# Where the last blocks of a Mamba layer hand over to its scans: order of work, an immediate finish, row-shaped decays, and square sums in a shared bank

## The chip, the cores and the metric

The kernel runs on one core of a Trainium2 chip. The metric is the device time of one execution in microseconds (us). Five engines work side by side and each takes its own instructions in order: TensorE (PE in the profile, PEld for its weight loads), VectorE (DVE), ScalarE (ACT), GpSimd (POOL) and SyncE (SP). SP, ACT and POOL also issue DMA transfers; in the profile these stand as SPq, ACTq and POOLq.

## The reference

Two layers over 1024 tokens of width 1024, each with a norm ahead of it and a residual, and a last norm. Layer A is a chunked causal spatial gating MLP, layer B a Mamba-2 mixer. The change lies in layer B:

```python
proj = h @ w_in
z, xbc, dt_raw = split(proj)
xbc = silu(causal_depthwise_conv(xbc, conv_w, conv_b))     # 4 taps
x, Bm, Cm = split(xbc)
dt = softplus(dt_raw + dt_bias);  dA_cs = cumsum(dt * A, axis=chunk)
decay = exp(where(causal, dA_cs[l] - dA_cs[s], -inf))
w_ls = (Cm @ Bm.T) * decay * dt
y_diag = w_ls @ x
states = Bm.T @ (exp(dA_cs[-1] - dA_cs) * dt * x)
state  = state * exp(dA_cs[-1]) + states                   # from chunk to chunk
y = y_diag + (Cm @ state_before) * exp(dA_cs) + x * d_skip
gated = rmsnorm_per_group(y * silu(z))                     # 8 groups of 256 channels
out = gated @ w_out
```

There are 8 groups of 4 heads of 64 channels, 128 states, and 8 chunks of 128 tokens. All is float32.

## The kernel before, in words

Every product in float32 is made of three passes (`mm3`, L134 to L136): an operand is split into a rounded part (`wh`, `hh`, a cast on ScalarE, L111) and a rest (`wl`, `hl`, a subtraction, mostly on VectorE, L112).

Most of layer B's input projection is done in blocks (`Block`), each a two by two product by Strassen-Winograd's scheme: seven smaller products in the order 1, 2, 6, 7, 5, 4, 3 instead of eight. A product needs one operand prepared (`prep`, which casts and subtracts), then TensorE fills a PSUM bank (tile `acc`), and `post` passes it on. Products 1, 6 and 7 are copied to `u` by ScalarE (L292), and the next product that goes on in the same bank waits for that copy. Products 2, 5, 4 and 3 complete the quarters C11, C22, C21 and C12, which go to the block's `done`.

The blocks of layer B are run by `blocks()`: a list `bs` of seven, of which the last is `zb[3]`, half as wide as the others (one unit for each product). For a z block, `done` adds on VectorE (L960), and a function `rest` applies SiLU on ScalarE (L965) and stores to `z_d` from ScalarE's queue (L966). C21 has no addition: its SiLU reads PSUM. For an xbc block, `done` puts a convolution into the list `todo`. A convolution is one activation on ScalarE (L1275), three taps on VectorE (L1269, with small extra taps at L1272 for the columns before), and as its `rest` a SiLU (L1300) and a store (L1301) on ScalarE.

`unit(b, n, i)` is one unit of a product. It takes what is in `late`, may pop one convolution from `todo` (whose `rest` goes into `late`), issues the matmuls and their `post`, and then runs what it took from `late`. So a SiLU normally comes one unit after the work that it needs. `finish()` runs all of `late` at once; before the change only block 0 calls it.

Four groups are not in blocks (`plain`: 2, 4, 6, 7). Their projections come from the generator `projections()`: straight products of four by two by two matmul triples into a double PSUM bank (`ab`). Its first `next` issues the first weight loads, then `prep(0, 0)` and `prep(0, 1)` split that weight, and the matmuls follow, two triples for each `next`. `prep` also issues the loads of the next weight, and from the second weight on subtracts on GpSimd.

`scans()` follows, with a new set of PSUM banks (`new_psum`): chunk by chunk and group by group, with pieces of the plain projections (`project`) between. In chunk n it issues `pe_b` of n (tiles `yy`, `sp`), `pe_a` of n + 2 (tile `tp`), then the updates, the weights of n + 1, the decay of n + 2, and the load of n + 3 (`wl<-cs_d`, one row of 4 heads by 128 to all partitions). `prefetch` loads half a group's x, B, C, its z, and in four DMAs the exponentials of the decays (`ze<-ecs_d`). For the group norm, `squares`, `sum_a`, `sum_b` and `sum_c` stand in the four chunks after a half is done: squares on ScalarE, a sum on GpSimd, sums over partitions on TensorE by a column of ones (tile `pr`, L1624) with a copy by ScalarE (tile `srow`, L1628), and a store by SP (L1631). The small PSUM tiles `yy`, `sp`, `tp` and `pr` share four banks.

The instructions inside `into_b()`, `blocks()` and `scans()` keep, on each engine, the order in which they are written (`tc.manual_schedule()`). What stands outside, such as the `next(pj)` between `blocks()` and `new_psum`, is placed by the scheduler at a time that it works out, and the lists of `blocks()` and `scans()` may also interleave where they meet.

Of the kernel before, what the change touches and what calls it, by code (L numbers as in the profile page):

```python
# [8 lines left out]
F32 = mybir.dt.float32  # L9
# [6 lines left out]
P = 128  # L16
T = 1024
# [6 lines left out]
NH = 32  # L24
# [5 lines left out]
def kernel(  # L30
# [921 lines left out]
    def z_block(b):  # L952

        wide = 256 if b < 3 else 128

        def done(name, i, a, u):
            th, j = 2 - int(name[1]), int(name[2]) - 1
            zt = k2([P, 512], "zt")
            if u is not None:
                nc.vector.tensor_tensor(out=zt, in0=a, in1=u, op=ALU.add)  # L960
                a = zt
            g, m = (2 * b + j, i) if b < 3 else (6, j)

            def rest():
                nc.scalar.activation(zt, a, AF.Silu)  # L965
                nc.scalar.dma_start(out=z_d[g][:, m, th * 512:(th + 1) * 512], in_=zt)  # L966

            late.append(rest)
            if not b:
                finish()  # L970

        def W(kh, j):
            c = 512 * b + j * wide
            return [b_w_in[kh * 512:(kh + 1) * 512, c:c + wide]]

        return Block(H2, W, False, done, None, wide)
# [31 lines left out]

    SPILT, AHEAD, LEFT = (0, 1, 3, 5), 16, 3
    zb = [z_block(b) for b in range(4)]  # L1010
# [181 lines left out]
    cs_d = dr.tile([8, NH, P], F32, name="cs_d")  # L1192
    ecs_d = dr.tile([8, NH, P], F32, name="ecs_d")

    def decays():
# [35 lines left out]
        for q in range(4):  # L1231
            rs_ = slice(q * 32, (q + 1) * 32)
            for sc, src in ((cs_d, cs), (ecs_d, ecs)):
                nc.sync.dma_start(out=sc[2 * q:2 * q + 2].rearrange("c h l -> h c l"),
                                  in_=src[rs_, :].rearrange("h (c l) -> h c l", c=2))
            yield
# [104 lines left out]
    def projections():  # L1341
# [37 lines left out]
        for kh in range(2):  # L1379
            prep(0, kh)  # L1380
        yield
        last = 0
        for i, (g, kind) in enumerate(seq):
            for m in range(2):
                drain(len(queue) - last)
                ab = acc2("ab")
                for kh in range(2):
                    for th in range(2):
                        for k in range(4):
                            mm3(ab[:, th, :], [w[:, k, m * P:(m + 1) * P] for w in W[i, kh]],  # L1390
                                [h_[:, k, :] for h_ in H2[f"A{2 - th}{kh + 1}"]], kh == 0 and k == 0,
                                kh == 1 and k == 3)
                            if (kh, th, k) == (1, 1, 3):
                                last = push(g, kind, m, ab)
                            if k % 2:
                                yield
                    if (m, kh) == (0, 1):
                        prep(i + 1, 0)
                    elif (m, kh) == (1, 0):
                        prep(i + 1, 1)  # L1400
# [3 lines left out]
    def blocks():  # L1404
# [11 lines left out]
        def unit(b, n, i):  # L1416

            turn[0] += 1
            off = late[:]
            late.clear()  # L1420
            if next(small, 0) == 0 and todo and (turn[0] % 2 or len(todo) > 3):
                late.append(todo.pop(0)())
            b.mm(n, i)
            for f in off:
                f()

        for at, (k, n) in enumerate(seq[1:], 1):
# [19 lines left out]
            elif n == 6:  # L1447
                next(pj)
            elif n == 7:
                next(a21)  # L1450
            elif n == 4:
                next(a21, None)
            for i in range(b.units):
                unit(b, n, i)
        while len(todo) > LEFT:
            convolve()

# [30 lines left out]
    def prefetch(g, th):  # L1488
# [8 lines left out]
        for f in range(2):  # L1497
            for pt in range(2):
                nc.sync.dma_start(
                    out=ze[f * 64:(f + 1) * 64, 2 + pt].rearrange("p (c l) -> p c l", c=4),  # L1500
                    in_=ecs_d[4 * th:4 * th + 4, 4 * g + 2 * pt + f, :].partition_broadcast(64))

    class Scan:
# [54 lines left out]

        def pe_b(self, c):
            w, wl = self.cw[c], self.wl.pop(c)  # L1560
# [5 lines left out]
            if c > 0:  # L1566
                for pt in range(2):
                    nc.tensor.matmul(out=yy[:, 256 + pt * P:384 + pt * P],  # L1568
                                     lhsT=self.state[c - 1][:, pt * P:(pt + 1) * P], rhs=self.x(3, c),
                                     start=True, stop=True)  # L1570
            sp = None
            if c < 7:
                sp = sm("sp")
                nc.tensor.matmul(out=sp[:, 0:256], lhsT=w[:, 512:640], rhs=w[:, 256:512], start=True, stop=True)
            self.ps[c] = yy, sp

# [41 lines left out]

        def sum_b(self):
            pr = sm("pr")  # L1620
            n = 1 if self.g < G - 1 else 2
# [62 lines left out]
    def scans():  # L1684
# [33 lines left out]
        for n, (g, c) in enumerate(chunks):  # L1718
            want = lambda f: AHEAD + (total - AHEAD) * (n + f) // N
            at("pe_b", n)  # L1720
            project(want(.5))
# [10 lines left out]
            at("load", n + 3)  # L1732
            p = g if c >= 4 else g - 1
            th = 0 if c >= 4 else 1
            if p >= 0:
# [3 lines left out]
                elif c % 4 == 1:  # L1739
                    sc.sum_a()  # L1740
                elif c % 4 == 2:
                    sc.sum_b()
                else:
                    sc.sum_c(th)
# [186 lines left out]
```

## Time and profile before

| | |
|---|---|
| median of 3 runs | 1622.55 us (1622.11 to 1625.1) |
| profiled execution | 1620.58 us, span 1618.9 us |
| TensorE busy | 1507.8 us (93%) |
| VectorE, ScalarE, GpSimd busy | 1056.2, 775.8, 458.4 us |
| DMA | 187256 packets, 259.17 MB |
| blocks of layer B | up to about 1050 us |
| scans with plain projections | about 1058 to 1400 us |

In a row of a timeline the columns are: start in us, duration in us, engine, line, operation, output tile <- input tiles, shapes, count. In brackets stands how long the engine was idle before the row and what, by the profile, ended that. A row with x2 or more merges several instructions, and its duration is theirs together. In a row of waits: who waited for whom, the total in us, how often, and the longest. A row of the table of windows gives the stretch, its length, the busy us (and instructions) of PE, PEld, DVE, ACT and POOL, then the granted TensorE clock as a share of full speed, the DMA share and GB/s.

### The profile page before, as it was taken

Reading aid. Unit: us, or ns where it says so; the run is one execution under the profiler, and the core shown is the slowest. Engines: PE = TensorE matmul, PEld = TensorE weight load, DVE = VectorE, ACT = ScalarE, POOL = GpSimd, SP = SyncE. Lnnn points to the kernel's source line nnn. Section 1 sums busy time; section 2 is a strip of 40 time slices with the busy share of each in tenths; the row PEclk is TensorE's granted clock in tenths of the full one; section 3 lists DMA queues with packets and bytes.
Section 4 is the critical chain, followed back from the end, with each engine's and each line's share of the span. In section 5 each row is a group of like instructions: output and inputs, shape, how many; then the busy total and the mean of one; then the engine's idle time right before and its main releaser. Section 6 shows DMA issues by size and latency. Waiting matters only on the chain.

```text
span 1618.9 us, 21275 instructions
## 1 busy us (share of the span) xinstructions
PE 1507.8 (93%) x7834; PEld 1241.1 (77%) x7834; DVE 1056.2 (65%) x1684; ACT 775.8 (48%) x1248; POOL 458.4 (28%) x466
## 2 busy tenths in 40 slices
PE   5799999999999999997999999889999999969987
PEld 5799988888888878775788787667767777747776
DVE  7966566666666545577737377747767667658656
ACT  4522233232323345554655555536666676444444
POOL 3601110000000131235311312026766666221231
PEclk8999999999999999998999999999999999979989
DMA  5153323323334999932377878766666765795992
GB/s 171 42 193 134 106 92 110 108 99 107 109 109 164 303 263 237 195 101 64 102 163 173 169 162 153 200 175 191 159 159 165 185 179 141 244 235 168 228 238 107
DMA packets 187256, 259.17 MB, mean 160 GB/s; under 512 B 16288, under 2 KB 117392, under 8 KB 183952
## 3 DMA queue, kind: packets, MB, share of 16 engines
q1 hardware_dynamic: 134144, 166.30, 34.0%
q0 software_dynamic: 39808, 70.53, 22.3%
q10 hardware_dynamic: 13200, 20.98, 3.6%
q8 instruction: 62, 1.02, 0.2%
q14 instruction: 42, 0.34, 0.1%
HBM read 183.52 MB, written 51.18 MB: 145 GB/s over the span
## 4 chain that ended last, share of the span: by engine, by line
PE 57%; issue 15%; DMA 10%; DVE 8%; ACT 7%; POOL 1%; SPq 1%; ACTq 0%; POOLq 0%; DVEq 0%
PE acc L136 10%; PE acc L134 9%; PE acc L135 9%; DMA wl<-cs_d 4%; PE ab L134 3%; PE ab L136 3%; PE ab L135 3%; PE ao L135 3%; PE ao L134 3%; PE ao L136 3%; PE yy L1564 2%; PE yy L1568 2%; DVE wl L112 2%; DVE xc L1269 2%; DMA wb<-in_b_w_out_dram 1%
## 5 line engine op out<-in xcount | busy, mean ns | idle before, releaser
L134 PE MATMUL acc<-hh,wh 128*128 128x512 f32 x868 | 343.4, 396 | 9.4 <-ACT wh L111 7.5
L136 PE MATMUL acc<-hh,wl 128*128 128x512 f32 x868 | 341.2, 393 | 4.9 <-DVE wl L112 4.8
L135 PE MATMUL acc<-hl,wh 128*128 128x512 f32 x868 | 340.1, 392 | 0.0
L112 DVE TENSOR_TENSOR wl<-wr,wh 128x1024 fp32r<-128x1024 f32 (+1 forms) x99 | 120.9, 1223 | 128.2 <-ACT wh L111 128.1
L134 PEld LDWEIGHTS acc<-hh,wh 128*128 128x128 f32 x868 | 164.5, 189 | 46.4 <-ACT wh L111 9.6
L136 PEld LDWEIGHTS acc<-hh,wl 128*128 128x128 f32 x868 | 164.4, 189 | 43.3 <-DVE wl L112 8.7
L135 PEld LDWEIGHTS acc<-hl,wh 128*128 128x128 f32 x868 | 164.5, 189 | 33.3
L111 ACT CAST wh<-wr 128x1024 fp32r<-128x1024 f32 (+1 forms) x113 | 116.4, 1030 | 98.0 <-PE acc L135 56.5
L292 ACT COPY u<-acc 128x512 f32<-128x512 f32 x117 | 67.7, 584 | 194.9 <-PE acc L136 193.7
L136 PE MATMUL acc<-wh,hl 128*128 128x256 f32 x448 | 130.2, 291 | 12.4 <-DVE hl L395 12.4
L134 PE MATMUL acc<-wh,hh 128*128 128x256 f32 x448 | 131.0, 292 | 3.8 <-DVE vt L331 2.5
L135 PE MATMUL acc<-wl,hh 128*128 128x256 f32 x448 | 129.6, 289 | 1.3 <-DVE wl L405 1.3
L134 PE MATMUL ab<-hh,wh 128*128 128x512 f32 x256 | 116.5, 455 | 8.7 <-ACT xc L1300 8.7
L1538 ACT ACTIVATE wl<-wl,tk 128x128 f32<-128x128 f32 x256 | 82.1, 391 | 84.9 <-DMA wl<-cs_d 84.5
L136 PE MATMUL ab<-hh,wl 128*128 128x512 f32 x256 | 101.6, 397 | 0.0
L135 PE MATMUL ab<-hl,wh 128*128 128x512 f32 x256 | 101.0, 395 | 0.0
L136 PEld LDWEIGHTS acc<-wh,hl 128*128 128x128 f32 x448 | 88.9, 198 | 13.5 <-DVE hl L395 13.5
L134 PE MATMUL bo<-wh,xh 128*128 128x512 f32 x192 | 80.5, 419 | 16.1 <-ACT xh L111 11.9
L134 PEld LDWEIGHTS acc<-wh,hh 128*128 128x128 f32 x448 | 88.8, 198 | 4.8 <-issue 2.9
L112 DVE TENSOR_TENSOR xl<-ya,xh 128x1024 fp32r<-128x1024 f32 x40 | 48.9, 1224 | 65.7 <-ACT xh L111 65.7
L135 PEld LDWEIGHTS acc<-wl,hh 128*128 128x128 f32 x448 | 88.8, 198 | 1.7 <-DVE wl L405 1.5
L111 ACT CAST xh<-ya 128x1024 fp32r<-128x1024 f32 x40 | 42.1, 1051 | 94.4 <-PE ao L135 43.0
(323 smaller groups left out, 3328.9 us busy)
## 6 DMA issues: line engine op xcount, KB each, us to landing
wr<-in_a_w_in_dram SPq DMA_DIRECT2D x48, 512.0 KB, 3.8
wl<-cs_d SPq DMA_DIRECT2D x64, 256.0 KB, 7.1
wr<-in_b_w_in_dram SPq DMA_DIRECT2D x30, 512.0 KB, 4.0
ya<-ya POOLq DMA_DIRECT2D x28, 512.0 KB, 15.0
wb<-in_a_w_out_dram SPq DMA_DIRECT2D x10, 1024.0 KB
wb<-in_b_w_out_dram SPq DMA_DIRECT2D x10, 1024.0 KB, 13.0
wr<-in_b_w_in_dram SPq DMA_DIRECT2D x36, 256.0 KB, 8.8
v<-v_d SPq DMA_DIRECT2D x8, 1024.0 KB, 4.8
```

What stands on the lines that cost most here:

```text
L111: nc.scalar.copy(out=hi, in_=src)
L112: return (eng or nc.vector).tensor_tensor(out=lo, in0=src, in1=hi.bitcast(F32), op=ALU.subtract)
L134: nc.tensor.matmul(out=o, lhsT=l[0], rhs=r[0], start=start, stop=False, **kw)
L135: nc.tensor.matmul(out=o, lhsT=l[0], rhs=r[1], start=False, stop=False, **kw)
L136: nc.tensor.matmul(out=o, lhsT=l[1], rhs=r[0], start=False, stop=stop, **kw)
L292: nc.scalar.copy(out=self.u[n][:, i], in_=a)
L1269: nc.vector.scalar_tensor_tensor(dst[:, s:], src[:, :n - s], convw(3 - s, ch), dst[:, s:], ALU.mult, ALU.add)
L1538: nc.scalar.activation(wl[:, j, :], wl[:, j, :], AF.Relu, scale=-1.0, bias=tokc(2, c, self.g)[:, j:j + 1])
L1564: nc.tensor.matmul(out=yy[f * 64:(f + 1) * 64, pt * P:(pt + 1) * P], lhsT=w[:, j * 64:(j + 1) * 64], rhs=wl[:, j, :], start=True, stop=True)
L1568: nc.tensor.matmul(out=yy[:, 256 + pt * P:384 + pt * P], lhsT=self.state[c - 1][:, pt * P:(pt + 1) * P], rhs=self.x(3, c), start=True, sto ...
```

## The change

There are five edits.

- `finish()` is now also called for z block 3, so that each of its four `rest` functions, and whatever else is in `late`, is issued at once.
- In the last block's products 4 and 3 no convolution is popped, and the loop that emptied `todo` down to three at the end of `blocks()` is gone. What is left is issued by the loop in `scans()`.
- `projections()` yields after each of the first two splits, and `blocks()` calls it once more at the last block's product 3, so the first split of the first plain weight is now issued there, in the written order. The second split stays at the `next(pj)` after the blocks. The two halves of the tokens are multiplied in the order 1, 0 instead of 0, 1.
- `ecs_d` is laid out as one row of 1024 for each head. Each load of `prefetch` now takes one run of 512 values instead of four runs of 128.
- `sum_b` is called from `pe_b` of the next chunk and puts its sums into the upper half of the state's bank (`sp`) instead of a bank of its own. In chunk 7, which has no state, `sp` is taken for it.

```diff
@@ z_block
             late.append(rest)
-            if not b:
+            if b in (0, 3):
                 finish()
@@ layer B
-    SPILT, AHEAD, LEFT = (0, 1, 3, 5), 16, 3
+    SPILT, AHEAD = (0, 1, 3, 5), 16
...
-    ecs_d = dr.tile([8, NH, P], F32, name="ecs_d")
+    ecs_d = dr.tile([NH, T], F32, name="ecs_d")
@@ decays
-            for sc, src in ((cs_d, cs), (ecs_d, ecs)):
-                nc.sync.dma_start(out=sc[2 * q:2 * q + 2].rearrange("c h l -> h c l"),
-                                  in_=src[rs_, :].rearrange("h (c l) -> h c l", c=2))
+            nc.sync.dma_start(out=cs_d[2 * q:2 * q + 2].rearrange("c h l -> h c l"),
+                              in_=cs[rs_, :].rearrange("h (c l) -> h c l", c=2))
+            nc.sync.dma_start(out=ecs_d[:, q * 256:(q + 1) * 256], in_=ecs[rs_, :])
@@ projections
         for kh in range(2):
             prep(0, kh)
-        yield
+            yield
...
-                    for th in range(2):
+                    for th in (1, 0):
...
-                            if (kh, th, k) == (1, 1, 3):
+                            if (kh, th, k) == (1, 0, 3):
                                 last = push(g, kind, m, ab)
@@ blocks
-            if next(small, 0) == 0 and todo and (turn[0] % 2 or len(todo) > 3):
+            if b is bs[-1] and n in (4, 3):
+                pass
+            elif next(small, 0) == 0 and todo and (turn[0] % 2 or len(todo) > 3):
                 late.append(todo.pop(0)())
...
             elif n == 4:
                 next(a21, None)
+            elif n == 3:
+                next(pj)
             for i in range(b.units):
                 unit(b, n, i)
-        while len(todo) > LEFT:
-            convolve()
@@ prefetch
-                nc.sync.dma_start(
-                    out=ze[f * 64:(f + 1) * 64, 2 + pt].rearrange("p (c l) -> p c l", c=4),
-                    in_=ecs_d[4 * th:4 * th + 4, 4 * g + 2 * pt + f, :].partition_broadcast(64))
+                h = 4 * g + 2 * pt + f
+                nc.sync.dma_start(out=ze[f * 64:(f + 1) * 64, 2 + pt],
+                                  in_=ecs_d[h, th * 512:(th + 1) * 512].partition_broadcast(64))
@@ Scan.pe_b
-        def pe_b(self, c):
+        def pe_b(self, c, ends=None):
...
+            if c < 7 or ends is not None:
+                sp = sm("sp")
             if c < 7:
-                sp = sm("sp")
                 nc.tensor.matmul(out=sp[:, 0:256], lhsT=w[:, 512:640], rhs=w[:, 256:512], start=True, stop=True)
+            if ends is not None:
+                ends.sum_b(sp[:, 256:512])
@@ Scan.sum_b
-        def sum_b(self):
-            pr = sm("pr")
+        def sum_b(self, pr=None):
+            pr = sm("pr") if pr is None else pr
@@ scans
-            at("pe_b", n)
+            p = g if c >= 4 else g - 1
+            at("pe_b", n, scan[p] if c % 4 == 3 and p >= 0 else None)
...
-                elif c % 4 == 2:
-                    sc.sum_b()
-                else:
+                elif c % 4 == 3:
                     sc.sum_c(th)
```

More of the change, by code (lines that the diff above doesn't have):

```diff
@@ L1732, in scans @@
             at("load", n + 3)
-            p = g if c >= 4 else g - 1
             th = 0 if c >= 4 else 1
```

## The prediction

> **What bounds the kernel now.** I read the page's span and busy times first, then TensorE's own waits, then the timeline around the two places that the change touches.
>
> ```profile
> span 1618.9 us, 21275 instructions
> PE 1507.8 (93%) x7834; PEld 1241.1 (77%) x7834; DVE 1056.2 (65%) x1684; ACT 775.8 (48%) x1248; POOL 458.4 (28%) x466
> ...
> 1040.00:1058.00 18.00, 9.38 (x39) 6.71 (x37) 14.58 (x22) 10.22 (x14) 2.83 (x1) 0.90 1.07 325
> ...
> PE ab L134 <- ACT xc L1300: 8.7, 1, 8.7
> ```
>
> TensorE is busy for 93% of the span, so time is only to be had where it stands still. The table of windows has one such stretch: in 1040 to 1058, TensorE works 9.38 of 18 us (first pair of numbers) while VectorE works 14.58 (third). The waits of TensorE there name one stop of 8.7 us, ahead of the first plain projection (tile `ab`). The releaser named, a SiLU of ScalarE, writes no PSUM; VectorE's rows show the real one:
>
> ```profile
> 1046.78 1.91 ACT L111 CAST hh<-f 128x2048 fp32r<-128x2048 f32 x1 [2.77 <-DMA f<-f_d]
> ...
> 1048.72 2.29 DVE L112 TENSOR_TENSOR hl<-f,hh 128x2048 fp32r<-128x2048 f32 x1 [1.52 <-ACT hh L111]
> 1050.93 2.35 DVE L112 TENSOR_TENSOR wl<-wr,wh 128x1024 fp32r<-128x1024 f32 x2
> 1053.32 2.72 DVE L1269 SCALAR_TENSOR_TENSOR xc<-u,par,xc 128x511 f32<-128x511 f32 x1
> ...
> 1057.66 0.68 DVE L960 TENSOR_TENSOR zt<-acc,u 128x512 f32<-128x512 f32 x1
> ...
> 1058.49 0.77 PE L134 MATMUL ab<-hh,wh 128*128 128x512 f32 x1 [8.68 <-ACT xc L1300]
> 1059.06 0.63 PE L135 MATMUL ab<-hl,wh 128*128 128x512 f32 x1
> ...
> 1061.19 0.45 PE L134 MATMUL ab<-hh,wh 128*128 128x512 f32 x1
> 1061.47 0.40 PE L135 MATMUL ab<-hl,wh 128*128 128x512 f32 x1
> 1061.71 0.40 PE L136 MATMUL ab<-hh,wl 128*128 128x512 f32 x1
> ```
>
> The last product of the blocks ended at 1049.8. Its reader L960 ends at 1058.34 and `ab` starts 0.15 later, in the PSUM that L960 frees. L960 stands on VectorE behind the split of A21, two weight splits and one convolution. The first six matmuls of `ab` take 2.70 us (1058.49 to 1061.19) where six at the later step of about 0.23 take 1.4: a slow clock adds 1.3.
>
> **The change at the seam, step by step.** With no convolution in products 4 and 3, the last convolution (from 1053.32 to L960, 4.3 us of VectorE) goes behind the first `ab` products. Its cost there is nothing, and what hides it is VectorE's idle time:
>
> ```profile
> 1072.24 3.92 DVE L1269 SCALAR_TENSOR_TENSOR x<-ab,par,x 128x1023 f32<-128x1023 f32 x3 [13.89 <-ACT x L1275]
> ```
>
> 13.9 us stand empty there; without them it would cost its 4.3 us. Its SiLU and store go the same way on ScalarE; group 5 reads it much later. The moved split `prep(0, 0)` issues one cast, one VectorE subtract and two SyncE loads, now ahead of product 3's reader, as they already stood; `prep(0, 1)` is free to fall behind L960, and is needed only 24 matmuls (5.4 us) into `ab`. The order (1, 0) of the halves saves nothing: A21 is split by 1051.0, before `ab` could start. By these steps alone L960 would follow the first split: 1048.72 + 2.29, half of 2.35, 0.68, so 1052.9, and `ab` would start at 1053.0, 5.5 us sooner.
>
> Against this stands the `finish()` for block 3. It runs everything in `late` at once, and that includes the SiLU of the convolution just issued in the same unit. ScalarE is in order, so it now stands still until VectorE has made the three taps. What is queued behind it there:
>
> ```profile
> 1034.35 0.62 ACT L1300 ACTIVATE xc<-xc 128x512 f32<-128x512 f32 x1
> ...
> 1035.37 0.62 ACT L111 CAST wh<-wr 128x512 fp32r<-128x512 f32 x1 [0.40 <-ACT xc L1300]
> 1035.90 0.81 ACT L1275 ACTIVATE xc<-u,par 128x512 f32<-128x512 f32 x1
> 1036.61 0.59 ACT L292 COPY u<-acc 128x512 f32<-128x512 f32 x1
> 1037.10 0.64 ACT L1300 ACTIVATE xc<-xc 128x512 f32<-128x512 f32 x1
> ...
> 1038.19 0.63 ACT L965 ACTIVATE zt<-zt 128x512 f32<-128x512 f32 x1 [0.46 <-DVE wl L112]
> ...
> 1039.22 0.62 ACT L111 CAST wh<-t 128x512 fp32r<-128x512 f32 x1 [0.40 <-ACT zt L965]
> ...
> 1034.48 2.31 DVE L1269 SCALAR_TENSOR_TENSOR xc<-acc,par,xc 128x511 f32<-128x511 f32 x3 [0.51 <-ACT xc L1275]
> 1036.72 0.68 DVE L960 TENSOR_TENSOR zt<-acc,u 128x512 f32<-128x512 f32 x1
> ...
> 1037.25 0.50 PE L134 MATMUL acc<-hh,wh 128*128 128x512 f32 x1 [0.68 <-ACT u L292]
> ```
>
> These are units 2 and 6 of the last z block. Today's order is: SiLU of an older convolution, cast for product 7, convolution, copy `u` (L292, which releases product 7 at 1037.25), and only then the SiLU of unit 2's convolution and of z. After the change it is: SiLU of unit 2's convolution (taps end 1036.79, so 1036.89), z's SiLU one step of 1.09 later (1037.98), the older SiLU (+1.03, 1039.01), the cast (+1.02, 1040.03), convolution (+0.53), copy (+0.71, 1041.27, done 1041.86). Product 7 starts at 1041.9 instead of 1037.25: **4.65 us late**, and after 5 us of standing still its first seven matmuls are slow (as after the stop at 1058).
>
> From there the chain is ScalarE and VectorE alone. Product 7 is done at 1046.2 (seven steps of 0.43, four of 0.23, 0.39); copy 0.5, SiLU 1.0, cast 0.5, convolution 0.8 bring the taps of unit 5 to 1049.15. Those taps last
>
> ```profile
> 1043.54 0.75 DVE L1269 SCALAR_TENSOR_TENSOR xc<-u,par,xc 128x511 f32<-128x511 f32 x1
> ...
> 1045.79 0.22 DVE L1272 SCALAR_TENSOR_TENSOR xc<-halo,par,xc 128x3 f32<-128x3 f32 x1
> ```
>
> 2.47, so to 1051.6. Then the second wait in line: SiLU 1051.7, z's SiLU 1052.8, cast for product 3 1053.85, cast of A21 1054.35 to 1056.25, its subtract 2.29 to 1058.6, the first split 1.18 to 1059.75, L960 0.68, `ab` at **1060.5**. That is 2.0 later than 1058.49, although the convolution is gone; 0.7 later if `ab` then starts at full clock. TensorE's stop there would be 2.7 us, behind another of 2.8 ahead of product 3. Rows for whether shorter stops slow the clock:
>
> ```profile
> 1014.77 0.50 PE L134 MATMUL acc<-hh,wh 128*128 128x512 f32 x1 [1.48 <-ACT wh L111]
> ...
> 1016.03 0.50 PE L136 MATMUL acc<-hh,wl 128*128 128x512 f32 x1 [0.53 <-DVE wl L112]
> ...
> 1017.18 0.63 PE L134 MATMUL acc<-hh,wh 128*128 128x512 f32 x1
> ```
>
> Stops of 1.48 and 0.53 were followed by slow matmuls too, so I give the slow clock 6 in 10 and take +1.5 for the seam. The ends are -5.5 (the waits in line cost nothing) and +3.7 (below).
> The Trainium skill (TensorE: Matmul & The Clock Gate, Part 1: The HAM clock gate) has TensorE fall to half clock after an idle window of about 3.4 us. By that rule a stop of 2.7 us leaves it warm and the seam is +0.7; the row at 1017.18 does not agree with it, and I keep +1.5.
>
> **The change in the scans.** Here TensorE has two stops of about 3 us. One of them, with SyncE's queue ahead of it:
>
> ```profile
> 1063.85 0.94 SPq L1527 DMA_DIRECT2D wl<-cs_d  x2
> ...
> 1194.36 2.60 SPq L1499 DMA_DIRECT2D ze<-ecs_d  x4
> 1197.06 0.55 SPq L1527 DMA_DIRECT2D wl<-cs_d  x1
> ...
> 1197.20 0.60 PE L1624 MATMUL pr<-gsq,ones 128*1 128x256 f32 x4
> ...
> 1204.83 1.28 ACT L1538 ACTIVATE wl<-wl,tk 128x128 f32<-128x128 f32 x4 [8.32 <-DMA wl<-cs_d]
> ...
> 1206.80 0.69 DVE L1556 TENSOR_TENSOR wl<-wl,cw 128x512 f32<-128x512 f32 x1 [4.57 <-ACT wl L1540]
> 1206.82 0.73 ACT L1628 COPY srow<-pr 1x256 f32<-1x256 f32 x2
> ...
> 1207.59 0.72 PE L1564 MATMUL yy<-wl,cw 128*64 128x128 f32 x8 [3.41 <-ACT srow L1628]
> ...
> 1294.86 0.66 PE L1564 MATMUL yy<-wl,cw 128*64 128x128 f32 x8 [2.94 <-ACT srow L1628]
> ...
> DMA to landing us min/median/max: 6.7/7.1/23.5
> ```
>
> The profile names the copy of the square sums, ended at 1207.55. But the weights of the same products ended at 1207.49, behind a decay that waited 8.32 us for its load. So moving the sums into the state's bank is worth 0.06 us at each of the stops it is named for: 0.2 in all, taken as nothing. It adds no wait here: the new place is behind the products that end near 1201.5, five before the copy. Elsewhere the copy may make ScalarE wait some tenths, covered by a decay that runs a chunk ahead; unhidden over 14 sums that would be up to 3.
>
> What counts is the load: it left SyncE at 1197.06, behind four `ecs_d` loads of 0.65 us each. One row of 2 KB per partition is the form of the `cs_d` loads, 0.47 each (0.94 for two). Four save 0.7. The load landed after 7.8; the last row, of the `cs_d` loads, has 6.7 at best and 7.1 in the middle; I take 7.1, so another 0.7. Ends: 0 (nothing lands sooner) and 0.7 + 1.1 = 1.8. Two stops times 1.4 are **-2.8**; next late is still the same load, since 3.41 - 1.4 leaves 2.0. The smaller copies into `ecs_d` lie among the blocks and change nothing.
>
> **Sum.** +1.5 - 2.8 - 0.2 = -1.5. Against the profiled execution (1620.58, of which 1618.9 is span) that is 1619.1; the median of the runs shown stands 1.97 above it, so **1621.0**.
>
> **Rivals.** (a) The waits in line are hidden and the seam closes as its first steps say: -5.5 - 3.0, 1614.0, and 1.3 less with a warm clock. For it: removing the 4.3 us is certain. Against it: L292 stands behind the SiLUs on an in-order engine. (b) The merged rows do not land or issue sooner: the seam alone, 1622.55 + 1.5 = 1624.0. For it: the cs_d loads, already in this form, still need 6.7 at best. The Trainium skill (DMA: Bandwidth & Descriptors, Specifications) calls 512 B enough for line rate, which speaks for this. (c) Slower: `prep(0, 1)`, which is outside the hand-written order, is placed ahead of A21's cast or of L960. Two casts and splits already stand before L960 today (2.35 for two), so it costs a cast of 1.0 and a split of 1.2 on the chain: seam +3.7 to +4.2. It decides once the loads give less than 0.5; with none, 1626.5.
>
> **Chances.** My forecast 0.60 (own range 1618 to 1624), (a) 0.17, (b) 0.13, (c) 0.10. No change is what lies within 0.2% (3.2 us), about what a measurement can tell. A fifth of the first case, where both loads land 1.8 sooner, lies below 1619.3 and counts with (a): faster 0.29, slower 0.10, same 0.61. The range goes to (a) with a slow or half warm clock, 1613.5, and nearly to (c), 1626.0.
>
> **What would show it.** Right: in the last z block a stop of about 5 us ahead of product 7, released by L292, with ScalarE waiting on a tap; `ab` near 1060; `ecs_d` issues near 0.47; the two stops in the scans at 1.5 to 2.0; the copy no longer named. Wrong: product 7 still near 1037 and `ab` near 1053, or the stops in the scans unchanged.

## The result and the profile after

| | before | after |
|---|---|---|
| median of 5 runs | 1622.55 us (1622.0 to 1626.07) | 1616.14 us (1611.99 to 1624.39) |
| ratio of the runs, 95% interval | | 0.9948 [0.9932, 0.9964] |
| profiled execution, span | 1620.58, 1618.9 us | 1619.06, 1617.4 us |

The changed kernel is faster by 0.5%. The forecast was 1621.0 us, with a chance of 0.61 for no change beyond 0.2% and of 0.29 for faster. The time lies inside the range as a whole (1613.5 to 1626.0) but below the 1618 to 1624 of the forecast's own case, and by the forecast's own 0.2% it is faster. The profiled execution of after is one of the longer of its five: it is 1.5 us shorter than that of before, where the medians are 6.4 us apart. The page of after:

```profile
span 1617.4 us, 21264 instructions
PE 1510.1 (93%) x7834; PEld 1243.0 (77%) x7834; DVE 1059.3 (65%) x1684; ACT 775.4 (48%) x1248; POOL 460.4 (28%) x466
...
DMA packets 174840, 259.17 MB, mean 160 GB/s; under 512 B 16288, under 2 KB 100880, under 8 KB 171536
```

Work and bytes are the same as before; only packets fell, from 187256, by the merged rows of `ecs_d`.

The seam, from TensorE's timeline of after (the bracket is the stop ahead of the row):

```profile
1015.81 0.50 PE L134 MATMUL acc<-hh,wh 128*128 128x512 f32 x1 [1.17 <-ACT wh L111]
...
1041.32 0.80 PE L134 MATMUL acc<-hh,wh 128*128 128x512 f32 x1 [4.84 <-ACT u L292]
...
1055.07 0.50 PE L134 MATMUL acc<-hh,wh 128*128 128x512 f32 x1 [2.47 <-ACT wh L111]
...
1061.04 0.75 PE L134 MATMUL ab<-hh,wh 128*128 128x512 f32 x1 [2.67 <-DVE zt L960]
...
1231.78 0.48 PE L1567 MATMUL yy<-wl,cw 128*64 128x128 f32 x2 [2.37 <-ACT wl L1542]
...
1317.95 0.66 PE L1567 MATMUL yy<-wl,cw 128*64 128x128 f32 x8 [1.86 <-ACT wl L1542]
```

One stop of 8.7 us ahead of `ab` has become three, of 4.84, 2.47 and 2.67 us, ahead of product 7, product 3 and `ab`. From the restart of TensorE near 1015 us, which both traces have (1014.77 before, 1015.81 after), `ab` starts 45.23 us later where it was 43.72. Part of this is not the change: up to the end of product 6 (the start of product 7 less its stop) that stretch takes 20.67 us in after and 21.80 in before, where some matmuls behind the restart follow each other at the slow step. Kernels with the same code up to there show both lengths. So the seam is measured from the end of product 6 below: `ab` starts 24.56 us behind it where it was 21.92, and the seam is 2.6 us longer in this profile. In the scans, the stops of 3.41 and 2.94 us are gone and two others are there. ScalarE's timeline of after shows why the seam's stops are where they are:

```profile
1036.32 0.63 ACT L1300 ACTIVATE xc<-xc 128x512 f32<-128x512 f32 x1 [2.44 <-DVE xc L1269]
...
1037.40 0.63 ACT L965 ACTIVATE zt<-zt 128x512 f32<-128x512 f32 x1 [0.46 <-ACT xc L1300]
...
1038.43 0.63 ACT L1300 ACTIVATE xc<-xc 128x512 f32<-128x512 f32 x1 [0.40 <-ACT zt L965]
...
1040.70 0.56 ACT L292 COPY u<-acc 128x512 f32<-128x512 f32 x1
...
1052.29 0.63 ACT L1300 ACTIVATE xc<-xc 128x512 f32<-128x512 f32 x1 [2.60 <-DVE xc L1272]
```

ScalarE waits 2.44 us for the taps of the convolution that was issued in the same unit; three SiLUs then stand ahead of the copy `u` (L292), and product 7 follows that copy. At 1052.29 the same happens once more.

The timeline of all engines of after shows, in the scans, a wait that the prediction did not have:

```profile
1225.31 0.60 PE L1630 MATMUL sp<-gsq,ones 128*1 128x256 f32 x4
...
1227.00 1.28 ACT L1540 ACTIVATE wl<-wl,tk 128x128 f32<-128x128 f32 x4 [9.25 <-DMA wl<-cs_d]
...
1228.99 0.73 ACT L1634 COPY srow<-sp 1x256 f32<-1x256 f32 x2
...
1229.81 0.42 DVE L1597 TENSOR_TENSOR state<-sp,state 128x256 f32<-128x256 f32 x1 [5.63 <-ACT srow L1634]
...
1230.99 0.69 DVE L1558 TENSOR_TENSOR wl<-wl,cw 128x512 f32<-128x512 f32 x1
```

The state's products were done when TensorE went on to the sums at 1225.31, but VectorE's update of the state (L1597) starts only behind ScalarE's copies of the square sums, which now lie in the same bank. Those copies stand behind a decay that waited 9.25 us for its load. The next weights (L1558) stand behind the update, and TensorE stops 2.37 us for them. VectorE's waits of after in the scans (1080 to 1400 us), in us: total, how often, longest:

```profile
DVE state L1597 <- PE sp L1578: 34.7, 25, 2.5
DVE state L1597 <- ACT srow L1634: 22.6, 6, 5.6
```

The second row has no counterpart in before.

### The profile page after: what moved, and what is told of

Same layout as the page of the kernel before. It is cut to its first block, busy times and chain, and to the rows that moved or that the text cites. A ratio compares the mean times of both kernels' runs of the same rounds, so it can differ in the third digit from the quotient of the medians.

```text
span 1617.4 us, 21264 instructions
## 1 busy us (share of the span) xinstructions
PE 1510.1 (93%) x7834; PEld 1243.0 (77%) x7834; DVE 1059.3 (65%) x1684; ACT 775.4 (48%) x1248; POOL 460.4 (28%) x466
## 4 chain that ended last, share of the span: by engine, by line
PE 53%; issue 17%; DMA 10%; DVE 9%; ACT 7%; POOL 2%; ACTq 1%; SPq 1%; POOLq 0%; DVEq 0%
PE acc L136 10%; PE acc L134 10%; PE acc L135 10%; DMA wl<-cs_d 4%; PE ab L134 3%; PE ab L136 3%; PE ab L135 3%; DMA ya<-ya 2%; PE yy L1567 2%; PE yy L1571 2%; DVE wl L112 2%; ACT wh L111 1%; PE bo L135 1%; PE sp L1578 1%; PE bo L134 1%
## 5 line engine op out<-in xcount | busy, mean ns | idle before, releaser
L292 ACT COPY u<-acc 128x512 f32<-128x512 f32 x117 | 67.7, 583 | 201.1 <-PE acc L136 199.8
```

The lines of the kernel that those rows point to most:

```text
L292: nc.scalar.copy(out=self.u[n][:, i], in_=a)
```

## The experiments

Theories. T1: the change's three parts act by themselves: the rows of `ecs_d` gain far more than forecast, the square sums in the shared bank cost (the update waits for the copies), and at the seam the gain of the moved convolution is spent by `finish()`. Rival R1: the sums are harmless and the rows gain little; the difference lies in the seam or in the scatter. For the rows: the gain comes from the length of a run, or from where the runs lie.

Before was run again beside each group of experiments: its median was 1623.05 us beside the first four, 1628.81 beside the next four, 1623.55 beside the last. TensorE's restart near 1015 us lies between 1012.7 and 1022.1 in the profiled executions. So I go by ratios, and inside a profile by stages that begin at a mark of their own. (A quotient of two medians differs from the measured ratio by up to 0.003, and lies inside its interval.) In this table the seam runs from the end of product 6 in the last z block to the start of the first `ab`, the next column from the end of product 6 to the first `yy`, which takes in a slow clock behind the start of `ab`, and the scans run from the first `yy` to the first `bo`. The last column is TensorE's stop ahead of a `bo` product near the scans' end (at 1430.01 in before). All are read from TensorE's timelines, one profile each. How far one profile can be trusted is seen in the two of the changed kernel: they differ by 1.1 us in the seam and 2.4 in the scans.

| kernel | ratio to before | seam, us | to first `yy`, us | scans, us | stop at `bo`, us |
|---|---|---|---|---|---|
| before | 1 | 21.92 | 46.35 | 323.96 | 8.70 |
| after | 0.9948 | 24.56 | 49.28 | 325.55 | 4.00 |
| after, again | 0.9949 | 23.47 | 46.60 | 323.13 | 2.81 |
| rows alone | 0.9917 | 20.86 | 45.91 | 317.50 | 5.76 |
| rows padded alone | 0.9937 | 21.28 | 46.07 | 316.41 | 5.32 |
| `finish()` alone | 1.0048 | 29.27 | 54.61 | 322.56 | 8.68 |
| sums alone | 1.0029 | 21.85 | 47.49 | 328.35 | 8.68 |
| seam alone, no `finish()` | 0.9976 | 16.38 | 41.12 | 322.70 | 8.70 |
| after, no `finish()` | 0.9942 | 16.96 | 41.72 | 321.95 | 5.54 |
| after, no sums | 0.9921 | 23.44 | 46.54 | 315.99 | 5.18 |
| after, copies behind | 0.9917 | 23.49 | 46.61 | 317.19 | 4.39 |
| after, neither | 0.9890 | 18.62 | 44.19 | 315.47 | 5.11 |
| after, no `finish()`, copies behind | 0.9907 | 18.10 | 43.93 | 320.49 | 5.36 |
| after, no sums, `finish()` twice | 0.9911 | 18.19 | 42.80 | 314.62 | 4.30 |

**One part alone, on the kernel before.** First `finish()`:

```diff
-            if not b:
+            if b in (0, 3):
                 finish()
```

> The kernel before with finish() for block 3 as well, all else as before. Theory (waits in line): product 7 starts 4 to 5 us late and ab another 2 to 4 us later than that chain gave in the changed kernel, since the last convolution is still ahead of it: 5 to 8 us slower, ratio 1.003 to 1.005. Rival: no change, since the seam's stop of 8.7 us takes up the delay.

1632.84 us, 1.0048 [1.0032, 1.0065], as expected. TensorE's timeline of this kernel:

```profile
1046.12 0.79 PE L134 MATMUL acc<-hh,wh 128*128 128x512 f32 x1 [5.29 <-ACT u L292]
...
1059.67 0.50 PE L134 MATMUL acc<-hh,wh 128*128 128x512 f32 x1 [2.75 <-ACT wh L111]
...
1070.10 0.77 PE L134 MATMUL ab<-hh,wh 128*128 128x512 f32 x1 [5.75 <-ACT xc L1300]
```

The two stops come with `finish()` alone, and the seam is 7.4 us longer. Its cost is not tied to the other edits.

The rows alone:

```diff
-    ecs_d = dr.tile([8, NH, P], F32, name="ecs_d")
+    ecs_d = dr.tile([NH, T], F32, name="ecs_d")
...
+                nc.sync.dma_start(out=ze[f * 64:(f + 1) * 64, 2 + pt],
+                                  in_=ecs_d[h, th * 512:(th + 1) * 512].partition_broadcast(64))
```

> The kernel before with the row-shaped ecs_d alone. Theory (the loads of the scans land sooner and the two stops of 3.4 and 2.9 us shrink): 3 to 7 us faster, ratio 0.9955 to 0.998, with the landing of the cs_d loads some tenths to 1 us shorter in the middle. Rival (512 B runs are moved as well as 2 KB runs): no change, and the two stops stay.

1612.94 us, 0.9917 [0.9885, 0.9949]: about 13 us by the ratio, far more than the 2.8 us of the sum and more than the 3 to 7 us expected here. Both stops of the scans are gone, not shortened, and the scans are 6.5 us shorter. The stop ahead of `bo` went from 8.70 to 5.76 us as well, a place that I had not counted.

The sums alone:

```diff
+            p = g if c >= 4 else g - 1
+            at("pe_b", n, scan[p] if c % 4 == 3 and p >= 0 else None)
...
+            if ends is not None:
+                ends.sum_b(sp[:, 256:512])
```

> The kernel before with the square sums in the state's bank alone. Theory (the copy named in the waits was only just the last): within 1 us of before, the stops of 3.4 and 2.9 us stay and are now put down to the weights. Rival (the bank was the wait): 7 us faster, the stops are gone.

1627.66 us, 1.0029 [1.0007, 1.005]: slower, and a miss. VectorE's waits in its scans, and then TensorE's timeline:

```profile
DVE state L1594 <- ACT srow L1631: 18.0, 5, 6.0
```

```profile
1240.70 0.66 PE L1564 MATMUL yy<-wl,cw 128*64 128x128 f32 x8 [2.00 <-ACT wl L1540]
...
1327.92 0.48 PE L1564 MATMUL yy<-wl,cw 128*64 128x128 f32 x2 [2.73 <-ACT wl L1540]
```

The new wait and its two stops come with this part, and R1's harmless sums fall.

The seam's other edits alone, that is the split moved ahead, the turned halves and no convolutions in products 4 and 3:

```diff
-        yield
+            yield
...
-                    for th in range(2):
+                    for th in (1, 0):
...
+            if b is bs[-1] and n in (4, 3):
+                pass
...
+            elif n == 3:
+                next(pj)
...
-        while len(todo) > LEFT:
-            convolve()
```

> The kernel before with the seam's edits alone, but finish() called for block 0 alone: no convolution behind the last products, the first plain weight split by two steps of prep, the th loop turned; ecs_d and the square sums as before. If the seam's gain is what the stage showed without finish() (from the restart of TensorE near 1015 us to the first ab: 37.6 us against 43.7) and the scans stay as they were, with their stops of 3.4 and 2.9 us: 0.9955 to 0.997 of before, and no stop of product 7. If the gain of the version without finish() was a matter of the other two parts: 0.999 to 1.001.

1619.8 us, 0.9976 [0.9958, 0.9994]. The estimate lies just outside the 0.9955 to 0.997 that I gave, its interval on both sides of that bound. By the stage, the seam is 5.5 us shorter (16.38 against 21.92), and product 7 has no long stop (0.68 us, as in before); the two stops of the scans (3.33 and 1.98 us) are, as they should be.

**The changed kernel with a part taken out.**

```diff
-            if b in (0, 3):
+            if not b:
                 finish()
```

> The changed kernel with finish() for block 0 alone, all else as changed. Theory (the SiLUs that wait in line cost the seam): the stop ahead of product 7 of the last z block shrinks from 4.84 us to under 1, product 3 waits no more for its cast, and ab starts 6 to 8 us sooner against the stretch before it than in the changed kernel; the time falls 6 to 8 us below the changed kernel's, ratio to before 0.990 to 0.992. Rival (those waits are hidden, the gain comes from the seam's other edits): the same as the changed kernel, 0.995.

1615.39 us, 0.9942 [0.9921, 0.9962]. The total misses what I expected, since it can't be told from after's; the seam does not miss: 16.96 us against 24.56. In the trace of this run product 7 has no long stop (0.68 us), and `ab` follows a stop of 4.01 us. The scans still have the sums' wait (22.1 us over six times). The same removal in a kernel without the sums' move, below, is plainer.

> The changed kernel, unaltered, as the mark for the three others beside it. Every theory: ratio to before 0.993 to 0.997; VectorE's state update waits for the copies of the square sums at six places, and TensorE has two stops of about 2 us there.

1619.91 us, 0.9949 [0.9931, 0.9967], the ratio that was expected. The update waits for the copies at six places again (19.0 us in all, 4.3 at most), but the two stops are 1.06 and 0.86 us, not about 2. The scans are long even so, 323.13 us, so those two stops are only a part of what the sums cost.

The square sums left where they were:

```diff
-            if ends is not None:
-                ends.sum_b(sp[:, 256:512])
...
-        def sum_b(self, pr=None):
-            pr = sm("pr") if pr is None else pr
+        def sum_b(self):
+            pr = sm("pr")
...
+                elif c % 4 == 2:
+                    sc.sum_b()
```

> The changed kernel with the square sums in their own bank, as before; finish() for block 3 stays. Theory (VectorE's state update waits behind the copies): 3 to 5 us faster than the changed kernel, the two stops of about 2 us gone; ratio to before 0.991 to 0.993. Rival (a difference of 4 us between single profiles is scatter): the same as the changed kernel.

1612.22 us, 0.9921 [0.9894, 0.9949], as expected by the ratio; by the medians of the two, run beside each other, 7.7 us are saved, more than the 3 to 5 expected. The scans take 315.99 us and no update waits for a copy.

The sums kept in the state's bank, but ScalarE's copies issued behind VectorE's update:

```diff
-                nc.scalar.copy(out=self.sr[h * 64:h * 64 + 1], in_=pr[h * 64:h * 64 + 1, 0:256])
...
+            if c % 4 == 3 and p >= 0:
+                scan[p].sum_copy()
```

> The changed kernel, with the sums still in the state's bank but ScalarE's two copies issued behind VectorE's state update instead of ahead of it. Theory (the wait is the update behind the copies in one bank): the waits of the update for the copies are gone, and the time is that of the kernel without the sums' move, 3 to 5 us below the changed kernel. Rival (the loss is in TensorE's order, with the sums ahead of pe_a): the same as the changed kernel.

1612.54 us, 0.9917 [0.9885, 0.9949]: not to be told from the kernel without the move. TensorE's order is that of the changed kernel, so the rival falls. The timeline of all engines of this kernel at the same update:

```profile
1219.46 0.60 PE L1630 MATMUL sp<-gsq,ones 128*1 128x256 f32 x4
...
1220.18 0.42 DVE L1597 TENSOR_TENSOR state<-sp,state 128x256 f32<-128x256 f32 x1 [1.85 <-PE sp L1630]
...
1222.79 0.70 DVE L1558 TENSOR_TENSOR wl<-wl,cw 128x512 f32<-128x512 f32 x1 [1.35 <-ACT wl L1542]
1222.81 0.73 ACT L1637 COPY srow<-sp 1x256 f32<-1x256 f32 x2
```

The update starts right behind TensorE's sums (1219.46 + 0.60), and the copies come 2.6 us later. That the update stood behind the copies was the cost, as far as the time can tell. The profiles leave a remainder open: in all six with the sums in the shared bank TensorE has three to five small stops ahead of `yy` (0.6 to 0.7 us each, 0.5 with the copies behind), put down to `ab`, and none of the others has them. What releases them was not looked for.

Both taken out, `finish()` for block 3 and the sums' move, by the two diffs above:

> The changed kernel with finish() for block 0 alone and the square sums in their own bank, as before; the seam's other edits and the row-shaped ecs_d stay. Theory (the two undone edits are the dear ones: 7.5 us of seam and 3 to 4 us of scans): ab about 6 us sooner than before after the stretch ahead of it, no stop over 2.4 us in the scans; 9 to 11 us below the changed kernel, ratio to before 0.988 to 0.990. Rival (what is won at the seam or in the scans is stood out later at the last group's loads): no better than the changed kernel without finish, 0.994.

1608.33 us, 0.9890 [0.9863, 0.9917], the ratio as expected and the lowest of all. The seam misses: `ab` starts 3.3 us sooner than in before (18.62 against 21.92), not about 6. And both costs taken out with the sums kept in the state's bank, that is without `finish()` for block 3 and with the copies behind the update:

> The changed kernel without finish() for block 3, and with ScalarE's copies of the square sums issued behind VectorE's update of the state: the two costs taken out, all else kept. If the two are independent of each other, it stands to the changed kernel as the version without both does: 0.988 to 0.991 of before, no wait of the update for a copy, no stop of product 7. If moving the sums into the state's bank costs anything beyond the wait for the copies: 0.992 or more.

1609.38 us, 0.9907 [0.9878, 0.9936]: as expected, not to be told from the one before it. Its update waits for no copy and product 7 has no long stop. Its interval still takes in 0.992, so a small cost of the place itself is not excluded.

**Whether `finish()` costs wherever it stands.**

```diff
-            if b in (0, 3):
+            if not b or b == 3 and name in ("C21", "C12"):
                 finish()
```

> The changed kernel without the square sums' move, with finish() in block 3 for the products C21 and C12 alone (those behind which product 3 and ab wait for nothing else), not for the others. If the in-line finish costs only where ScalarE's next evacuation stands behind it, product 7 starts without a stop, and ab comes some 0.6 us sooner than with none (its stop of 4.0 us ended at zt, whose SiLU stood behind three casts): 0.987 to 0.990 of before. If finish() costs wherever it stands: a stop of 2 us or more at product 3 or 7 and 0.990 to 0.993.

1606.41 us, 0.9911 [0.9882, 0.994], which does not tell the two bands apart. The profile does: product 7 starts after 0.67 us, product 3 after 0.41, and the stop ahead of `ab` has another releaser. TensorE's timeline of this kernel, then that of the version with neither:

```profile
1037.89 0.50 PE L134 MATMUL acc<-hh,wh 128*128 128x512 f32 x1 [0.67 <-ACT u L292]
1047.39 0.47 PE L134 MATMUL acc<-hh,wh 128*128 128x512 f32 x1 [0.41 <-DVE zt L960]
1055.41 0.77 PE L134 MATMUL ab<-hh,wh 128*128 128x512 f32 x1 [4.92 <-ACT wh L111]
```

```profile
1062.10 0.79 PE L134 MATMUL ab<-hh,wh 128*128 128x512 f32 x1 [5.35 <-ACT zt L965]
```

So the call costs where a copy or a cast that TensorE needs stands behind it, at C11 and C22 (products 2 and 5), and not at the last two. It brings nothing that can be told there: the seam takes 18.19 us, where the four kernels without the call have 16.38 to 18.62. C21's SiLU comes ahead of three casts, but `ab` then waits for its weight.

**Why the rows gain.** The layout by heads, but each chunk padded, so that a load still takes four runs of 512 B:

```diff
-    ecs_d = dr.tile([8, NH, P], F32, name="ecs_d")
+    ecs_d = dr.tile([NH, 8, 160], F32, name="ecs_d")
...
-                    in_=ecs_d[4 * th:4 * th + 4, 4 * g + 2 * pt + f, :].partition_broadcast(64))
+                    in_=ecs_d[h, 4 * th:4 * th + 4, 0:P].partition_broadcast(64))
```

> The kernel before with ecs_d laid out by heads as in the changed kernel, but each chunk's 128 values padded to 160, so that a load still comes as four runs of 512 B for each partition and not as one of 2 KB; the store writes 512 B runs too. If the gain of the rows comes from the length of the run (fewer packets): packets as before, about 187,000, the loads land as late as before (7 to 8 us), the stops of 3.4 and 2.9 us stay, 0.998 to 1.002 of before. If it comes from where the rows lie (a head's chunks side by side): landing about 6 us, stops gone, 0.990 to 0.994.

1612.76 us, 0.9937 [0.991, 0.9964], and the stops of the scans are gone. Its page has before's packets:

```profile
span 1606.2 us, 21275 instructions
...
DMA packets 187256, 259.17 MB, mean 161 GB/s; under 512 B 16288, under 2 KB 117392, under 8 KB 183952
```

So the gain, as far as the two intervals can tell, is not in fewer or longer packets but in where the runs lie: the four runs of a load are 32 x 128 x 4 = 16384 B apart in before and 640 B here. (The stores into `ecs_d` lie otherwise too; that the loads make the gain is read from the queue, not from a run of its own.) SyncE's timeline shows it at the first stop; before first, behind the `ecs_d` loads shown in the prediction, then this kernel:

```profile
1197.65 2.04 SPq L120 DMA_DIRECT2D wr<-in_b_w_in_dram  x2
1199.80 2.62 SPq L1527 DMA_DIRECT2D wl<-cs_d  x2
```

```profile
1190.68 2.59 SPq L1501 DMA_DIRECT2D ze<-ecs_d  x4
1193.37 0.55 SPq L1529 DMA_DIRECT2D wl<-cs_d  x1
1193.97 0.98 SPq L120 DMA_DIRECT2D wr<-in_b_w_in_dram  x2
1195.06 0.91 SPq L1529 DMA_DIRECT2D wl<-cs_d  x2
```

The `ecs_d` loads themselves are issued in the same 2.6 us. What differs is what comes behind them: two weight loads take 2.04 against 0.98 us to issue, two decay loads 2.62 against 0.91. And the first decay load lands sooner. ScalarE's timeline of the padded kernel has its reader:

```profile
1198.14 1.28 ACT L1540 ACTIVATE wl<-wl,tk 128x128 f32<-128x128 f32 x4 [5.32 <-DMA wl<-cs_d]
```

From issue to reader that is 1198.14 - 1193.37 = 4.8 us, against 1204.83 - 1197.06 = 7.8 before. The seam alone, with before's layout, has 7.7 (issued 1195.07, read 1202.76); the unpadded rows have 5.2 (1195.84, 1201.04). Near the end it is more. SyncE's timelines, before and then the padded kernel, behind the last group's `ecs_d` loads:

```profile
1393.34 2.60 SPq L1499 DMA_DIRECT2D ze<-ecs_d  x4
...
1397.72 4.62 SPq L702 DMA_DIRECT2D wb<-in_b_w_out_dram  x2
1402.43 5.74 SPq L1794 DMA_DIRECT2D ya<-g_d  x1
```

```profile
1383.29 2.61 SPq L1501 DMA_DIRECT2D ze<-ecs_d  x4
...
1387.68 1.22 SPq L702 DMA_DIRECT2D wb<-in_b_w_out_dram  x2
1388.99 0.85 SPq L1796 DMA_DIRECT2D ya<-g_d  x1
```

There the same three issues took 10.4 us and take 2.1 (4.62 + 5.74 against 1.22 + 0.85). Later issues of the padded kernel are slow again (a decay load 4.48 us, two of `ya` 6.13), so not all of the 8.3 us is won. It goes with the shorter stop ahead of `bo`: in the table's last column every kernel with the scattered layout has 8.68 to 8.70 us, and every one with the layout by heads 2.81 to 5.76. Whether the distance or its being a power of two holds the loads up was not tried, and neither was the same for `cs_d`.

## Why the prediction was right or wrong

The sum gave -1.5 us, and the profiled execution after is 1.5 us shorter. That is no confirmation: two terms were wrong by much and against each other, and this execution is among the longer ones. By the medians the change is worth -6.4 us, by the ratio about 8.4 (0.0052 x 1622.55).

- **The seam was right by its steps.** Forecast: stops of about 5, 2.8 and 2.7 us, released by L292, a cast and L960; measured: 4.84, 2.47 and 2.67 with these releasers. Taken apart, the stage is 3.3 to 5.5 us shorter than in before where `finish()` is left out (the first steps gave 5.5), and `finish()` puts 4.8 to 7.6 back in the four pairs of kernels of the table that differ in it alone. Over the whole kernel the parts have the same signs: 0.9976 and 1.0048.
- **The slow clock came as forecast in this profile, and in no other of this seam.** The forecast of +1.5 weighed two cases, +2.0 with a slow clock at `ab` and +0.7 without. From the table of windows of after (the last three numbers are the granted clock, the DMA share and GB/s):

```profile
1061.00:1063.70 2.70, 2.66 (x6) 2.14 (x7) 2.70 (x1) 0.91 (x2) 2.12 (x1) 0.51 0.87 350
```

The clock was 0.51 behind a stop of 2.67 us, and from the end of product 6 to the first `yy`, with the slow start of `ab` in it, after takes 2.9 us longer than before. Three other profiles have the same seam (after again, no sums, copies behind), and in them the slow matmuls came one product earlier. TensorE's timeline of the kernel without the sums' move:

```profile
1053.73 0.50 PE L134 MATMUL acc<-hh,wh 128*128 128x512 f32 x1 [2.74 <-ACT wh L111]
...
1054.45 0.80 PE L136 MATMUL acc<-hh,wl 128*128 128x512 f32 x1
...
1059.68 0.47 PE L134 MATMUL ab<-hh,wh 128*128 128x512 f32 x1 [1.19 <-DVE zt L960]
```

Product 3 turns slow from its third matmul on. It then ends later, `ab` waits 1.2 us instead of 2.67 and starts at full speed, and to the first `yy` the three take 0.2 to 0.3 us longer than before. So the seam's term, the clock included, was +0.2 to +0.3 in three profiles and +2.9 in one; that +1.5 lies between them is in part luck. The rule weighed in the prediction (the Trainium skill, TensorE: Matmul & The Clock Gate, Part 1: The HAM clock gate: about 3.4 us idle) would have left it at full speed if only that stop counted; the trace does not agree with that reading of it. It is not the length alone: behind 2.47 us at 1055.07 in after the fourth matmul already started 0.24 us ahead of the next, and behind 2.74 us the clock fell only 0.7 us after TensorE had gone on. At the scans' stop of 2.37 us the state's two products (L1578) took 1.06 us where they took 0.60 at 1224.78, so such stops cost more than their length.
- **The convolution moved behind costs nothing**, as said: from the first `ab` to the first `yy`, where it now stands (VectorE, from 1064.12 in after), after takes 24.72 us and before 24.43; kernels with the move take 23.10 to 25.83 us there, those without 24.43 to 25.64.
- **The step that failed by size: the rows, -2.8.** The term had 0.7 for the issue and 0.7 for the landing at each of two stops, with a floor of 6.7 us taken from the `cs_d` loads. The issue did not get shorter: four `ecs_d` loads take 2.51 us in after against 2.60. The landing got shorter by 2.6 to 3.0 us, below the floor, because that floor was itself measured behind the scattered loads. So the stops did not shrink to 2.0; they went. (The stops of 2.37 and 1.86 us in after look like the forecast's 1.5 to 2.0, but they are others, made by the sums.) And the queue behind the last group, which I had left out, gave another 3 to 6 us ahead of `bo`. Measured: about -13 us [-19, -8] for the rows alone, -10 [-15, -6] padded (ratio less one, times 1623). I took the size of a run for what mattered. The Trainium skill (DMA: Bandwidth & Descriptors, Specifications) has 512 B as enough for line rate, and the padded kernel, with runs of 512 B and 0.9937, agrees that the length is not it.
- **The step that failed by kind: "it adds no wait here".** I asked whether ScalarE's copy would wait for TensorE, and it doesn't. I did not ask who else reads the bank. VectorE's update does, and it waited for the copies, up to 5.6 us, six times. I allowed up to 3 us, unhidden, for the wrong engine; the cost is about +4.7 us [+1.1, +8.1]. The Trainium skill (PSUM — Partial Sum Buffer, PSUM bank collisions raise a hardware error) says that the compiler's scheduler adds a dependency between instructions of any two engines that touch the same bank and quadrant, two readers included. The trace agrees with such a dependency, with an update that reads other columns than the copies.
- **Rivals.** (a) gave 1614.0, nearest to the median, but for a reason that did not happen: the waits in line were not hidden. The small part of the chance for faster that named loads landing 1.8 us sooner had the cause that was measured. (b) and (c) did not occur; (b)'s premise that the rows land no sooner is the opposite of what was measured.

Together the parts close roughly: rows 0.9917, sums +0.0029, seam with `finish()` about +1.5 us (0.0009, from the stage) make 0.9955, where 0.9948 and 0.9949 were measured. With the seam's own ratios in place of the stage (0.9976 and 1.0048) they make 0.9970; the intervals of the four parts, 0.002 to 0.003 to each side, take in both.

Both costs removed, the kernel stands at 0.9890 of before, about half a per cent below the change as made. The profile of that version still has a stop of 5.35 us ahead of `ab`: C21's SiLU behind casts, and those behind the cast of A21, which waited 3.78 us for its load.

## What to carry to other kernels

Before a function that "runs what is pending at once" is called on an in-order engine, list what is queued behind the youngest item in it; here the stops came with the two calls that have a copy or a cast for TensorE behind them, and none with the two that have not. Before two results share a PSUM bank, list the readers of both on every engine: a late, unimportant copy on one can hold the urgent reader on the other, and issuing it behind the urgent one brought the time back to that of the kernel with two banks. And a load's price is also what it does to the transfers behind it in its queue: look at the issue times of the next rows, not at its own.

## What the runs showed of the hardware

A broadcast load of four 512 B runs that lie 16384 B apart held up the transfers issued behind it. With the runs 640 B apart, and the same packets and bytes, the next load was read 4.8 us after its issue instead of 7.8, and two issues later in the same queue took 0.91 us instead of 2.62 (1.52 with the rows alone). I had taken a transfer's cost from its run length and its own issue time, and both were the same.

The TensorE clock fell to 0.51 behind a stop of 2.67 us that followed another of 2.47 by 3.3 us of work; behind the first of the two the matmuls followed each other at full speed from the fourth on. In three other profiles of the same code up to there the first stop was 2.73 to 2.77 us; there the matmuls behind it were slow from the third on, and those behind the second stop, of 1.2 us, ran at full speed. So stops of the same code below 3 us are followed by a slow clock in one execution and not in another.
